# Later turns, a later first head and attention squares in SBUF in a hybrid decoder layer on one core

## The chip, the cores and the metric

The kernel runs on one NeuronCore of one Trainium2 chip. Its five instruction engines are named as in the profile: PE (TensorE, matrix products), DVE (VectorE), ACT (ScalarE), POOL (GpSimd) and SP (SyncE, which issues most DMAs). The metric is the device time of one execution in microseconds (us). Times are medians of several runs, and the profile is of one more execution.

## The reference

One decoder layer on 1024 tokens of width 1024, all in float32. A first RMS norm feeds one input projection, whose columns are split between two groups of heads:

```python
h = rms_norm(x, norm1_w[l])
proj = h @ w_in[l]
da_q, da_k, da_v, dn_qkv, dn_z, dn_a, dn_b = jnp.split(proj, [...], axis=-1)

da_q = rms_norm(da_q.reshape(B, S, DA_HEADS, 2, DA_QK_DIM), q_norm_w[l])   # 4 heads, two maps of 64
da_k = rms_norm(da_k.reshape(B, S, DA_HEADS, 2, DA_QK_DIM), k_norm_w[l])
da_o = diff_attention(da_q, da_k, da_v, lam)       # (softmax(q1 k1^T) - lam softmax(q2 k2^T)) v, causal
da_o = rms_norm(da_o, da_out_norm_w[l]) * (1.0 - lam_init)

dn_qkv = causal_conv_silu(dn_qkv, conv_w[l])       # group B: gated DeltaNet, 4 heads of 128
dn_o = gated_delta_rule(dn_q, dn_k, dn_v, g, beta) # chunked scan over the sequence
dn_o = rms_norm(dn_o, dn_out_norm_w[l]) * jax.nn.silu(dn_z...)

x = x + jnp.concatenate([da_o, dn_o], axis=-1) @ w_out[l]
h = rms_norm(x, norm2_w[l])
x = x + jnp.square(jax.nn.relu(h @ w_up[l])) @ w_down[l]
```

## The kernel before

The tokens are eight tiles of 128. Large products are made in float32 accuracy from rounded parts: each operand is split into a high part (`wH`, `hH`) and the rest (`wL`, `hL`), and three matmuls are added up. The kernel has four parts in time: norm, gates and convolution inputs up to about 226 us; an interleaved part up to about 600 us; the MLP's first matrix; the MLP's second.

The interleaved part is what the change touches. It runs these streams beside each other:

- `da_units()`: the projections of group A in six units of eight token tiles: keys, queries, values of heads 0 and 1 (`g` = 0), then of heads 2 and 3 (`g` = 1). A tile's product `ps_qk` is 24 matmuls (L1077 to L1079). For keys and queries ACT squares it (L1095) and copies it to `qn` (L1096), DVE sums the squares (L1098) and scales them (L290), POOL takes the power (L291), and DVE multiplies `qn` in place (L1102). The row is then put on the list `late`, with the time at which the planner expects it ready.
- `da_turns()`: takes the first of `late`, transposes it on PE into a PSUM bank (`ps_qkt`, L1038 and L1039), scales and splits it on ACT and DVE (`qa`, L1042 and L1043) and stores it to `qk_d` in DRAM by a DMA that POOL issues (L1044).
- `scan()` and `scan_out()`: the DeltaNet scan over eight chunks. A step has three groups of four products into `ps_A` (L928, L940, L951), with DVE or ACT between them (L932, L942, L957). `scan_out` makes a chunk's output from two more groups into one PSUM bank (`ps_o`, L980 and L987), evacuated by DVE (L981, L989). Operands come back from DRAM by SP's DMAs: `pka` (L920, two buffers), `pkb` (L970, five buffers, one per head) and `zgt` (L972). Its output goes out through POOL (`mixn_d`, L1001).
- `scores()`: loads a head's keys (`KS`, four DMAs, L1128), values (`vt`, L1135) and each tile's queries (`qa` and `qb`, four DMAs, L1143 and L1144), makes the scores `ps_sc` (L1203, L1204) and, on DVE and ACT, the two softmaxes `pexp` (L1214, L1215) and their difference (L1226).
- `values()`: transposes `pexp` (`ps_at`, L1248), copies it (L1250), multiplies by the values (`ps_o`, L1260), copies the result to `om` (L1269), squares that with a sum (L1270) and normalises it. The 32 outputs (4 heads, 8 tiles) each pass here.
- `mixed()`, `outproj()` and what follows: transposes of the mixed heads (`ps_tr`, L298), the output projection (`ps_op`, L1350 to L1352), the second norm.

The order on PE is written by a planner, the class `Interleave`, at build time. Each stream is a generator that yields the time from which it may go on, and the stream of the lowest priority number that may go on is run. Time moves on by assumed PE durations (`flow.pe`), and `flow.chain` books assumed durations on the other engines. PE's instructions stand in exactly this order (`tc.manual_schedule(engines={T.engine})`). The other engines' orders in this part, SP's DMA issues and POOL's among them, are not the planner's: the framework's scheduler makes them from the recorded program. At run time each engine works through its list in order and waits for what it needs.

Two PSUM banks, named `px`, are shared by the turned rows, the transposed `pexp`, the products with the values and the transposed mixed rows. The planner books a bank as free again after the copy that empties it. Before the change, the square of L1270 wrote its unused output into another part of the same bank, behind that copy:

```python
sq = po[:, P:2 * P]
S.copy(om, po[:, :P])
S.activation(sq, om, AF.Square, scale=ri[:, 0:1], accum_out=so)
...
t = flow.chain(act(P))
flow.hold(r, t)
```

Of the kernel before, what the change touches and what calls it, by code (L numbers as in the profile page):

```python
# [9 lines left out]
F32 = mybir.dt.float32  # L10
# [8 lines left out]
P = 128  # L19
# [12 lines left out]
MARGIN = 0.25  # L32
SCAN_START = 18000.0
MIX_T = 5000.0
DMA_T = 2500.0
AHEAD = 2

# [74 lines left out]
def vec(n, extra=0.0):  # L112
    return "V", 68.0 + 1.045 * n + extra


def powr(n):
    return "G", 180.0 + 285.0 * n
# [3 lines left out]
def tile_hymba_layer(  # L121
# [718 lines left out]
    for h, hf, q2 in skew(dn_proj(0)):  # L840
# [5 lines left out]
        sq = ta("kn", 2)  # L846
# [204 lines left out]
    def da_units():  # L1051
        todo = [(g, kind) for g in range(2) for kind in (1, 0, 2)]

        w = load_unit(w_units[2 * todo[0][1] + todo[0][0]]), unit_time()
        for g, kind in todo[1:]:
            quarters.plan(w_units[2 * kind + g])
        for k0 in (4, 0):
            for n in range(2):
                quarters.plan(w_halves[n], k0, 4)
        quarters.load()  # L1060
        quarters.load()
        freed = [0.0, 0.0]
        n = 0
        for i, (g, kind) in enumerate(todo):
            (wh, wl), wt = w
            for j in range(NT):
                tb = NT - 1 - j if i == len(todo) - 1 else j
                if j == 0:
                    if i + 1 < len(todo):
                        w = quarters.unit(256, KB)  # L1070
                    else:
                        pre.append(quarters.unit(512, 4))
                sl = slice(tb * P, (tb + 1) * P)
                yield max(freed[n % 2], wt[0] if j == 0 else 0.0), None
                ps = pj.tile([P, 512], F32, tag="pj", name="ps_qk")
                for k in range(KB):
                    T.matmul(ps[:, :256], hH[:, k, sl], wh[:, k, :], start=(k == 0), stop=False)  # L1077
                    T.matmul(ps[:, :256], hH[:, k, sl], wl[:, k, :], start=False, stop=False)  # L1078
                    T.matmul(ps[:, :256], hL[:, k, sl], wh[:, k, :], start=False, stop=(k == KB - 1))  # L1079
                    if k % 2 == 1:  # L1080
                        flow.pe(6 * TR)
                        if k < KB - 1:
                            yield wt[k // 2 + 1], None
                while len(late) > 2:
                    yield flow.now + 50, None
                qn = sd.tile([P, 256], F32, tag="qn", name="qn", bufs=4)
                if kind == 2:
                    newest["ACT"] = S.copy(qn, ps[:, :256])
                    st = nc.gpsimd.dma_start(v_d[g, tb], qn.rearrange("p (h e) -> p h e", h=2))
                    if g == 1:  # L1090
                        prefetch_x()
                    freed[n % 2] = flow.chain(act(256))
                else:
                    sq = ps[:, 256:512]
                    S.activation(sq, ps[:, :256], AF.Square)  # L1095
                    newest["ACT"] = S.copy(qn, ps[:, :256])  # L1096
                    sn = sd.tile([P, 4], F32, tag="sn", name="sn", bufs=2)
                    V.tensor_reduce(sn, sq.rearrange("p (a d) -> p a d", d=DQK), axis=AX.X, op=ALU.add)  # L1098
                    rn = sd.tile([P, 4], F32, tag="rn", name="rn", bufs=2)
                    rstd(rn, sn, 1.0 / DQK, EPS, sd, "rnt", 4)  # L1100
                    qv = qn.rearrange("p (a d) -> p a d", d=DQK)
                    V.tensor_tensor(qv, qv, rn.unsqueeze(2).broadcast_to([P, 4, DQK]), ALU.mult)  # L1102
                    t = flow.chain(act(256))
                    flow.chain(act(256), start=t - flow.HOP)
                    freed[n % 2] = t = flow.chain(vec(256), start=t - flow.HOP)
                    t = flow.chain(vec(4), powr(4), vec(256), start=t - flow.HOP)
                    late.append((g, kind, tb, qn, t))
                quarters.block()
                if i == len(todo) - 1:
                    over.add(tb)  # L1110
                n += 1
                state["units"] = n
            if kind == 2:
                while state["turned"] < 2 * NT * (g + 1):
                    yield flow.now + 50, None
                state["da"] = g + 1
                state["da_t"] = flow.now + 3000
        sdctx.close()
        pctx.close()
        state["proj"] = True  # L1120

    def load_head(h, pool):

        KS = []
        for m in range(2):
            k = pool.tile([P, SEQ], F32R, tag=f"KS{m}", name=f"KS{m}")
            for s in range(2):
                nc.sync.dma_start(k[HF[s]].bitcast(F32).rearrange("p (b t) -> p b t", t=P),  # L1128
                                  qk_d[h // 2, 1, :, HF[h % 2], s, m * P:(m + 1) * P].rearrange("b p t -> p b t"))
            KS.append(k)  # L1130
        return KS

    def load_v(h, pool):
        vt = pool.tile([P, NT, P], F32, tag="vt", name="vt")
        nc.sync.dma_start(vt, v_d[h // 2, :, :, h % 2, :].rearrange("t p e -> p t e"))  # L1135
        return vt
# [14 lines left out]
    def scores():  # L1151
        heads, npe, nsc = {}, 0, 0
        while state["da"] < 1:
            yield flow.now + 300, None
        heads[0] = load_head(0, ap), load_v(0, ap)
        q = load_q(*order[0])
        yield state["da_t"] + 3000, None
        for u, (h, tb) in enumerate(order):
            if u >= NT - 3 and 1 not in heads and state["scan"] or h == 1 and 1 not in heads:

# [71 lines left out]
    def values():  # L1232
        for _ in order:
            while not ready or ready[0][5] > flow.now:
                yield (flow.now + 100 if not ready else ready[0][5]), None
            h, tb, pe, ri, vt, _t = ready[0]
            if h == 2:
                while "ax" not in pools or len(rows_of) + len([x for x in loads if not x[3]]) > 1:
                    yield flow.now + 50, None
                rows_of[tb] = pools["ax"].tile([P, 512], F32, tag="mx", name="mx", bufs=2)  # L1240
                nc.sync.dma_start(rows_of[tb][:, 0:256], mixa_d[tb])
            ats = []
            for g in range(0, tb + 1, 4):
                r = yield from flow.bank("px")
                ng = min(4, tb + 1 - g)
                pt = bank_tile(px, r, "ps_at")
                for j in range(ng):
                    T.transpose(pt[:, j * P:(j + 1) * P], pe[:, (g + j) * P:(g + j + 1) * P], ident)  # L1248
                at = ap.tile([P, 512], F32, tag="at", name="at", bufs=2)
                newest["ACT"] = S.copy(at[:, :ng * P], pt[:, :ng * P])  # L1250
                ats.append(at)
                if g + 4 > tb:
                    ready.pop(0)
                flow.pe(ng * TR)
                t = flow.chain(act(ng * P))
                flow.hold(r, t)
            r = yield from flow.bank("px", at=t)
            po = bank_tile(px, r, "ps_o")
            for j in range(tb + 1):
                T.matmul(po[:, :P], ats[j // 4][:, (j % 4) * P:(j % 4 + 1) * P], vt[:, j, :],  # L1260
                         start=(j == 0), stop=(j == tb))
            if h < 2:
                om = ap.tile([P, P], F32, tag="om", name="om", bufs=2)
            else:

                om = rows_of[tb][:, h * P:(h + 1) * P]
            sq = po[:, P:2 * P]
            so = ap.tile([P, 1], F32, tag="so2", name="so2", bufs=2)
            S.copy(om, po[:, :P])  # L1269
            S.activation(sq, om, AF.Square, scale=ri[:, 0:1], accum_out=so)  # L1270
            f = ap.tile([P, 1], F32, tag="of2", name="of2", bufs=2)
            rstd(f, so, 1.0 / P, EPS, ap, "oft2", 1)
            V.tensor_tensor(f, f, ri[:, 0:1], ALU.mult)
            V.scalar_tensor_tensor(om, om, f, dawb, ALU.mult, ALU.mult)
            if h < 2:
                nc.gpsimd.dma_start(mixa_d[tb, :, h * P:(h + 1) * P], om)
            flow.pe((tb + 1) * MM)
            t = flow.chain(act(P))
            flow.hold(r, t)
            t = flow.chain(act(P, True), vec(1), powr(1), vec(1), vec(P, 60), start=t)  # L1280
            if h == 3:
                loads.append((rows_of.pop(tb), t, tb, 0))
        state["attn"] = True
# [644 lines left out]
```

## Time and profile before

| what | value |
|---|---|
| time, median of 3 runs | 1233.85 us (1232.64 to 1236.31) |
| time of the profiled execution | 1233.5 us |
| its span, first to last instruction | 1231.8 us |
| mean granted clock of PE | 0.998 |
| PE busy | 1215.3 us, 99% of the span |
| DVE, ACT, POOL busy | 829.9, 624.3, 151.3 us |
| data moved by DMA | 202.12 MB, mean 164 GB/s |

A row of waits reads: the waiting engine, the tile and line it was about to work on, an arrow, the engine, tile and line that released it, then the total in us, the number of times and the longest. A timeline row reads: start in us, duration in us, engine, line, operation, output tile and input tiles, and in brackets the idle time before it and what ended it. Matmuls are pipelined, so the durations of neighbours overlap. `SPq` is SP's queue of DMA issues. PE idle time is the complement of its busy time in a stretch.

### The profile page before, as it was taken

The page shows a single profiled execution, that of the slowest core. Times are in us where ns is not written, and L with a number is a line of the kernel's source. Part 1 is how long each engine was busy: PE and PEld are TensorE (multiplying, and loading weights), DVE is VectorE, ACT ScalarE, POOL GpSimd, SP SyncE. Part 2 cuts the span into 40 slices and gives each one's busy share as a digit, 9 for nine tenths or more (in the row PEclk, how much of TensorE's full clock was granted, in tenths as well). Part 3 has the DMA queues.
Part 4 walks back from the last instruction along what each step waited for, and adds up shares of the span by engine and source line. Part 5 has one row for each costly group of instructions (what it writes and reads, how often), then busy time and mean ns, then how long its engine had stood idle before and what let it go on. Part 6 is the DMA issues. An engine that isn't in the chain of part 4 may idle for free.

```text
span 1231.8 us, 18793 instructions
## 1 busy us (share of the span) xinstructions
PE 1215.3 (99%) x6791; PEld 1052.0 (85%) x6791; DVE 829.9 (67%) x1534; ACT 624.3 (51%) x1249; POOL 151.3 (12%) x215
## 2 busy tenths in 40 slices
PE   9999999998999999999999999999999999999998
PEld 8978888898999998888888888888888888888886
DVE  6868797665647657776799544565569755777543
ACT  6587553344356555566766544454564333333330
POOL 2411110033434421001200000000000000000000
PEclk9999999999999999999999999999999999999999
DMA  9334654378648855223437433444479655423401
GB/s 351 103 111 119 167 163 86 78 244 240 223 146 246 241 162 159 84 74 109 157 120 257 171 129 145 171 171 154 154 244 386 229 178 184 162 103 103 137 35 69
DMA packets 155973, 202.12 MB, mean 164 GB/s; under 512 B 37688, under 2 KB 110952, under 8 KB 155880
## 3 DMA queue, kind: packets, MB, share of 16 engines
q1 hardware_dynamic: 151256, 187.28, 46.9%
q0 software_dynamic: 4480, 13.64, 2.9%
q8 instruction: 54, 0.88, 0.3%
q14 instruction: 39, 0.32, 0.1%
q10 hardware_dynamic: 144, 0.00, 0.0%
HBM read 135.86 MB, written 65.01 MB: 163 GB/s over the span
## 4 chain that ended last, share of the span: by engine, by line
PE 90%; DMA 3%; DVE 2%; ACT 2%; issue 1%; SPq 1%; POOL 1%; DVEq 0%; ACTq 0%; POOLq 0%
PE X L1527 5%; PE X L1526 5%; PE X L1525 5%; PE X L1825 4%; PE X L1823 4%; PE X L1824 4%; PE ps_dn L265 3%; PE ps_dn L267 3%; PE ps_dn L266 3%; PE ps_qk L1077 3%; PE ps_qk L1079 3%; PE ps_qk L1078 3%; PE Y L1525 3%; PE Y L1526 3%; PE Y L1527 3%; PE ps_o L1260 2%
## 5 line engine op out<-in xcount | busy, mean ns | idle before, releaser
L1443 ACT CAST hH<-ur 128x1024 fp32r<-128x1024 f32 x56 | 58.9, 1051 | 173.4 <-PE Y L1824 89.4
L1444 DVE TENSOR_TENSOR hL<-ur,hH 128x1024 fp32r<-128x1024 f32 x56 | 68.4, 1223 | 78.9 <-ACT hH L1443 78.8
L1077 PE MATMUL ps_qk<-wH,hH 128*128 128x256 f32 x384 | 115.1, 300 | 0.0
L1079 PE MATMUL ps_qk<-wH,hL 128*128 128x256 f32 x384 | 109.0, 284 | 0.0
L1078 PE MATMUL ps_qk<-wL,hH 128*128 128x256 f32 x384 | 108.9, 284 | 0.0
L1444 DVE TENSOR_TENSOR op<-raw,op 128x1024 fp32r<-128x1024 f32 x48 | 58.7, 1224 | 74.1 <-PE X L1526 41.1
L1823 PE MATMUL X<-hH 128*128 128x512 f32 x224 | 87.1, 389 | 0.0
L1824 PE MATMUL X<-hL,hH 128*128 128x512 f32 x224 | 87.1, 389 | 0.0
L1825 PE MATMUL X<-hH,hL 128*128 128x512 f32 x224 | 87.1, 389 | 0.0
L265 PE MATMUL ps_dn<-hH,wH 128*128 128x512 f32 x192 | 76.0, 396 | 0.2 <-ACT cp L679 0.2
L266 PE MATMUL ps_dn<-hL,wH 128*128 128x512 f32 x192 | 75.8, 395 | 0.0
L267 PE MATMUL ps_dn<-hH,wL 128*128 128x512 f32 x192 | 75.5, 394 | 0.0
L1077 PEld LDWEIGHTS ps_qk<-wH,hH 128*128 128x128 f32 x384 | 74.0, 193 | 0.5 <-DVE sn L1098 0.2
L1078 PEld LDWEIGHTS ps_qk<-wL,hH 128*128 128x128 f32 x384 | 74.0, 193 | 0.2
L1079 PEld LDWEIGHTS ps_qk<-wH,hL 128*128 128x128 f32 x384 | 73.6, 192 | 0.0
L1444 DVE TENSOR_TENSOR hL<-dw,hH 128x1024 fp32r<-128x1024 f32 x56 | 68.2, 1219 | 1.4 <-ACT hH L1443 1.4
L1443 ACT CAST op<-raw 128x1024 fp32r<-128x1024 f32 x48 | 50.4, 1051 | 35.7 <-PE Y L1527 19.9
L1443 ACT CAST hH<-dw 128x1024 fp32r<-128x1024 f32 x56 | 58.7, 1049 | 10.9 <-DMA dw<-in_w_down_dram 5.5
L1215 ACT ACTIVATE pexp<-pexp,mx 128x128 f32<-128x128 f32 (+7 forms) x64 | 49.7, 777 | 24.5 <-DVE mx L1214 24.1
L683 DVE SCALAR_TENSOR_TENSOR cy<-cp,pv,cy 128x512 f32<-128x512 f32 x72 | 53.7, 747 | 8.4 <-ACT cy L681 7.5
L1350 PE MATMUL ps_op<-wH,hH 128*128 128x512 f32 x128 | 53.0, 414 | 0.0
L1352 PE MATMUL ps_op<-wH,hL 128*128 128x512 f32 x128 | 50.3, 393 | 0.0
(374 smaller groups left out, 3424.2 us busy)
## 6 DMA issues: line engine op xcount, KB each, us to landing
ur<-ud SPq DMA_DIRECT2D x28, 1024.0 KB, 5.3
raw<-in_w_up_dram SPq DMA_DIRECT2D x32, 512.0 KB, 4.2
dw<-in_w_down_dram SPq DMA_DIRECT2D x32, 512.0 KB, 6.5
wraw<-in_w_units_dram SPq DMA_DIRECT2D x48, 256.0 KB, 3.6
qk_d<-qa POOLq DMA_DIRECT2D x32, 256.0 KB, 4.2
ud<-ua SPq DMA_DIRECT2D x16, 512.0 KB, 4.3
ud<-s SPq DMA_DIRECT2D x16, 512.0 KB, 2.7
pka<-park_d SPq DMA_DIRECT2D x32, 192.0 KB, 4.3
```

The costliest lines, as they stand in the source:

```text
L265: T.matmul(ps, lh(k), rh(k), start=(k == 0), stop=False)
L266: T.matmul(ps, lh(k), rl(k), start=False, stop=False)
L267: T.matmul(ps, ll(k), rh(k), start=False, stop=(k == n - 1))
L1077: T.matmul(ps[:, :256], hH[:, k, sl], wh[:, k, :], start=(k == 0), stop=False)
L1078: T.matmul(ps[:, :256], hH[:, k, sl], wl[:, k, :], start=False, stop=False)
L1079: T.matmul(ps[:, :256], hL[:, k, sl], wh[:, k, :], start=False, stop=(k == KB - 1))
L1443: S.copy(dst[0], src)
L1444: V.tensor_tensor(dst[1], src, dst[0].bitcast(F32), ALU.subtract)
L1525: T.matmul(ps, op[0][:, k, cs], h[0][:, k, :], start=start and k == 0, stop=False, skip_group_check=True)
L1823: T.matmul(bank[t], v[0][:, j, sl], v[2][:, j], start=s0, stop=False, skip_group_check=True)
L1824: T.matmul(bank[t], v[0][:, j, sl], v[3][:, j], start=False, stop=False, skip_group_check=True)
L1825: T.matmul(bank[t], v[1][:, j, sl], v[2][:, j], start=False, stop=s1, skip_group_check=True)
```

## The change

Four edits in the interleaved part:

1. `late` may hold three rows, where it held two, before a unit's evacuation is recorded. There are four `qn` buffers before and after.
2. A row's planned time of readiness is put 1500 planner nanoseconds later (`TURN_T`).
3. After the first half of the projections is turned, `scores()` lets 4500 planner nanoseconds pass (`HEAD_T`) before it records the loads of the first head's keys, values and queries, and then 6000 more before the first scores. Before, it recorded the loads at once, and the first scores followed 3000 after `da_t`, which itself lies 3000 after the end of the turns.
4. The square of L1270 writes a new SBUF tile `osq2` of 128 x 128 with one buffer, instead of the PSUM bank.

```diff
 MIX_T = 5000.0
+TURN_T = 1500.0
+HEAD_T = 4500.0
 DMA_T = 2500.0
...
-                while len(late) > 2:
+                while len(late) > 3:
                     yield flow.now + 50, None
...
-                    t = flow.chain(vec(4), powr(4), vec(256), start=t - flow.HOP)
+                    t = flow.chain(vec(4), powr(4), vec(256), start=t - flow.HOP) + TURN_T
                     late.append((g, kind, tb, qn, t))
...
         while state["da"] < 1:
             yield flow.now + 300, None
+        yield flow.now + HEAD_T, None
         heads[0] = load_head(0, ap), load_v(0, ap)
         q = load_q(*order[0])
-        yield state["da_t"] + 3000, None
+        yield flow.now + 6000, None
...
-            sq = po[:, P:2 * P]
+            sq = ap.tile([P, P], F32, tag="osq2", name="osq2", bufs=1)
             so = ap.tile([P, 1], F32, tag="so2", name="so2", bufs=2)
             S.copy(om, po[:, :P])
             S.activation(sq, om, AF.Square, scale=ri[:, 0:1], accum_out=so)
```

## The prediction

> **What bounds the kernel.** I read the page first, then a table by stretches, then TensorE's own waits, and after that the chain and the timeline at the places that those waits name.
>
> ```profile
> span 1231.8 us, 18793 instructions
> PE 1215.3 (99%) x6791; PEld 1052.0 (85%) x6791; DVE 829.9 (67%) x1534; ACT 624.3 (51%) x1249; POOL 151.3 (12%) x215
> PE 90%; DMA 3%; DVE 2%; ACT 2%; issue 1%; SPq 1%; POOL 1%; DVEq 0%; ACTq 0%; POOLq 0%
> ...
> 226.00:364.00 138.00, 132.86 (x1160) 129.78 (x1159) 81.46 (x234) 57.47 (x168) 45.70 (x58) 0.99 0.62 192
> 364.00:460.00 96.00, 94.18 (x764) 92.11 (x763) 63.13 (x190) 59.49 (x165) 41.07 (x60) 1.00 0.71 215
> 460.00:600.00 140.00, 138.86 (x808) 120.39 (x807) 100.35 (x265) 86.33 (x224) 19.59 (x32) 1.00 0.35 104
> ```
>
> TensorE fills 99% of the span, so it is the bound, and no matmul is added or removed by this change (the built programs hold the same number of each). What can change is TensorE's idle time, and the change touches only the interleaved part, from about 226 to 600 us. Each row of the table is window, length, then busy time of PE, weight load, DVE, ACT and POOL, then clock, DMA share and GB/s. PE is idle for 138.00 - 132.86 = 5.1, 96.00 - 94.18 = 1.8 and 140.00 - 138.86 = 1.1 us: 8.1 us in all. That, and what a stop costs beside its idle time, is all that can be won.
>
> ```profile
> PE ps_o L980 <- DMA pkb<-park_d: 2.8, 1, 2.8
> PE ps_qkt L1038 <- DVE qn L1102: 1.8, 3, 1.0
> ...
> PE ps_qkt L1038 <- ACT ps_o L1270: 1.3, 2, 1.0
> ...
> PE ps_at L1248 <- ACT ps_o L1270: 0.8, 2, 0.7
> ...
> PE ps_sc L1204 <- DMA qb<-qk_d: 0.3, 1, 0.3
> PE ps_qkt L1038 <- DVE oft L290: 0.3, 1, 0.3
> ```
>
> These rows (total us, times, longest) name 7.3 of the 8.1 us. Three causes: a scan operand that lands late (2.8), normalised rows not ready when TensorE turns them (1.8 + 0.3: the row put down to `oft` is the turn of a late row too), and a PSUM bank still held by the attention's square (1.3 + 0.8).
>
> A stop costs more than its idle time, because matmuls overlap:
>
> ```profile
> 278.39 0.28 PE L1078 MATMUL ps_qk<-wL,hH 128*128 128x256 f32 x1
> 278.51 0.28 PE L1079 MATMUL ps_qk<-wH,hL 128*128 128x256 f32 x1
> 279.82 0.33 PE L1038 MATMUL ps_qkt<-ident,qn 128*128 128x128 f32 x1 [1.03 <-DVE qn L1102]
> ```
>
> Starts are 0.12 us apart, so the turn was due at 278.63 and came at 279.82: 1.19 us lost for 1.03 shown, 0.16 more per stop.
>
> **Rows planned later (TURN_T, three in waiting).** The planner puts 1.5 us more between a row's normalisation and its two transposes, and lets one more row queue (three, where two were allowed), so a unit need not wait at its end. In the built order of the changed program, the TensorE work between a unit's last matmul and its turn (rows 2 to 31, counted in matmuls times their start-to-start time in the trace: 0.12 us for a projection, 0.89 for a group of four scan products) is at least 6.26 us; before, it was at least 4.71. For the row above it was 18 projection matmuls, three scan groups and another turn, 4.95 us; now it is 36, three and one, 7.19 us. What it must cover is in the timeline:
>
> ```profile
> 273.47 0.28 PE L1079 MATMUL ps_qk<-wH,hL 128*128 128x256 f32 x1
> 277.63 0.60 POOL L1044 DMA_DIRECT2D qk_d<-qa  x1 [5.55 <-DVE rnt L290]
> 278.26 1.05 POOL L291 TENSOR_TENSOR rn<-rnt,neghalf 128x4 f32<-128x4 f32 x1
> 279.34 0.43 DVE L1102 TENSOR_TENSOR qn<-qn,rn 128x256 f32<-128x256 f32 x1
> ```
>
> The unit ended at 273.47, the row was ready at 279.77: 6.30 us, now under 7.19. The same count for the other late rows comes out safe too, the closest by a few tenths. So the four stops go: 1.8 + 0.3 + 4 x 0.16 = **2.7 us won**. Bounds: 0 (DVE and POOL come later by as much) to 2.7.
>
> **Squares in SBUF.** The square's output moves out of the bank, so the bank is free after the copy alone:
>
> ```profile
> 369.16 0.26 ACT L1269 COPY om<-ps_o 128x128 f32<-128x128 f32 x1
> 369.89 0.40 PE L1204 MATMUL ps_sc<-KS,qb 128*128 128x512 f32 x1
> 370.18 0.62 ACT L224 CAST wH<-wraw 128x512 fp32r<-128x512 f32 x1
> 370.70 0.37 ACT L1270 ACTIVATE ps_o<-om,ri 128x128 f32<-128x128 f32 x1
> 371.00 0.19 ACT L1270 ACTIVATION_READ_ACCUMULATOR ps_o<-om,ri 128x1 f32 x1
> 371.25 0.33 PE L1038 MATMUL ps_qkt<-ident,qn 128*128 128x128 f32 x1 [0.96 <-ACT ps_o L1270]
> ```
>
> The copy was done at 369.42, before TensorE wanted the bank at about 370.1; the square, behind a weight rounding on ACT, held it until 371.19. All four such stops end so: 1.3 + 0.8 + 4 x 0.16 = **2.7 us won**. Bounds: 0 (the copy or the next row is late instead) to 2.7. On ACT it costs this:
>
> ```profile
> L994 ACT ACTIVATE osq<-oc,small x32: 389/402/412, 261.5 to 350.4; 128x128 f32<-128x128 f32 x32
> L1270 ACT ACTIVATE ps_o<-om,ri x16: 366/372/377, 370.7 to 495.0; 128x128 f32<-128x128 f32 x16
> ```
>
> The scan's square of the same shape writes SBUF and takes a median of 402 ns, the attention's into PSUM 372. 32 squares x 30 ns = 1.0 us of ACT, which is busy 59 of 96 us in its fullest stretch. I take 0 on the path; bounds 0 to 1.0. The one buffer is written by ACT alone, in order, so nothing waits for it. The Trainium skill, "ScalarE: Activation LUTs" (its note that ScalarE to PSUM is faster than to SBUF), advises the opposite destination; the two rows above agree with its sign, and by it alone the edit would lose 1.0 us. Its own caveat, that TensorE must not need the PSUM, is what decides here.
>
> **First head's keys later (HEAD_T).** The wait it bears on is the dearest:
>
> ```profile
> 282.91 3.86 DMA qk_d<-qa
> 286.84 0.69 SPq L1128
> ...
> 288.92 0.63 SPq L1128
> ...
> 289.66 7.24 DMA pkb<-park_d
> 296.94 1.35 PE ps_o L980 x6
> ...
> DMA to landing us min/median/max: 2.1/4.3/6.8
> ...
> 297.00:298.30 1.30, 1.30 (x7) 1.18 (x8) 0.00 (x0) 0.00 (x0) 0.00 (x0) 0.82 0.93 296
> 298.30:301.30 3.00, 3.00 (x16) 3.00 (x16) 2.07 (x6) 0.38 (x2) 0.60 (x1) 0.51 0.44 148
> ...
> 280.50:284.00 3.50, 3.50 (x33) 3.50 (x32) 3.14 (x12) 1.01 (x3) 1.81 (x4) 1.00 0.99 360
> ```
>
> The last turned key row is stored at 282.91 and lands at 286.8; SP then issues the four key loads (L1128), and the scan's `pkb` loads behind them land 7.24 us after issue, where their median is 4.3. TensorE stops for 2.8 us (2.97 with the refill), and afterwards its granted clock is 0.51 for 3 us: 14 matmuls start 0.21 instead of 0.12 us apart or slower, about 1.4 us more. So this stop costs 4.4 us.
>
> But the delay is on the planner's clock, and only TensorE's order is taken from the planner. SP's is made by the scheduler. In the built order of the changed program the four key loads stand where they stood: after three groups of `pkb` and `zgt` loads, directly ahead of the four `pkb` loads of the same chunk. What moves is TensorE: the first score matmul comes after 672 projection matmuls instead of 636 (4.3 us later), and from the previous chunk's second product to this chunk's first there are 6.4 us of work instead of 5.7. The last key row is turned 2.2 us later by the order, of which 1.19 are the stop that goes; its store stands one normalisation further back on POOL. So keys and `pkb` land at about the same time as before, and TensorE wants them about 0.8 us later: I take a stop of 2.0 us, **0.8 us won**. Whether the clock still falls lies between two rows: after the 1.03 us of idle at 279.82 it stayed at 1.00 (last row), after 2.81 it fell. 2.0 is nearer to 2.81, so I leave the 1.4 us in. Bounds: 0 to 4.4.
>
> The Trainium skill, "TensorE: Matmul & The Clock Gate" (Part 1), says that the clock halves after an idle window of about 3.4 us. Here 2.81 us sufficed, so the measurement decides against that figure; by the rule a stop of 2.0 would keep the clock, which is rival 4.
>
> **New waits.** All streams are shuffled by a few us. In the built order six distances of the scan are short now: three times a chunk's second output product follows its first by 2.4 to 2.7 us (3.1 at the least before), and three times the next scan step follows by 3.1 to 3.3 (3.2 at the least before, mostly 4 to 6). They need DVE in time, which is busy 81 of 138 us there.
>
> ```profile
> 278.11 1.12 DVE L957 SCALAR_TENSOR_TENSOR S<-S,elast,ps_A 128x128 f32<-128x128 f32 x4 [0.71 <-PE ps_A L951]
> ```
>
> One such group ahead in DVE's queue is 1.1 us; I take one, **1.0 us lost**. Bounds: 0 to 6.6 (all six).
>
> **The sum.** 2.7 + 2.7 + 0.8 - 1.0 = 5.2 us won. The profiled execution took 1233.5 us (1.7 around its span), the median of the runs is 1233.85, 0.35 above. 1233.85 - 5.2 = **1228.6 us**. From about 440 us on the two TensorE orders hardly differ, and after 600 not at all. About 0.3%, 3.7 us, is what a measurement can tell from no change.
>
> **Rivals.**
> 1. The keys do get out of the way: `pkb` lands in time, and the clock holds. 2.7 + 2.7 + 4.4 - 1.0 = 8.8: 1225.0 us. For it: the stop is a matter of 2 us. Against: SP's order. That this edit does not do what it says stands in the forecast; here it does. Chance 0.15.
> 2. The waits come back elsewhere: 3 to 8 us of new stops, at the six tight places and at score, transpose and value products, which now start 4.3 us late and catch up within 20 us. 1230.6 to 1235.6, about 1232. For it: DVE and ACT are two thirds busy between 364 and 460. Against: the least distance before a turn grows by 1.5 us. Chance 0.22.
> 3. Slower: scan loads late. SP is in order; the first head's query loads, which wait for the ninth and tenth turned rows, stand ahead of the next chunks' loads, and the tenth comes 2.2 us later. If the first product (L980) of chunks 4 to 7 then stops as chunk 3's did, 4 x 3.0 = 12.0 us replace the 1.0: gain 6.2 - 12.0, so 1239.7 us. It decides from the fourth such stop (9.9 us of loss needed). Against: chunk 4's first product itself comes 4.8 us later in the order. Chance 0.13.
> 4. The forecast, but the clock holds through the shorter stop: 5.2 + 1.4 = 6.6, so 1227.2 us. For it: 1.03 us did no harm; against: 2.81 did. By the Trainium skill's "TensorE: Matmul & The Clock Gate" this is the outcome. Chance 0.09.
> 5. The forecast, with the 32 slower squares on the path: 5.2 - 1.0 = 4.2, so 1229.6 us. Against: none of TensorE's waits ends at the scan's squares. By the Trainium skill's "ScalarE: Activation LUTs" this is the direction. Chance 0.03.
>
> The forecast, 1227 to 1230.1, has the rest, 0.38. Range: 1224.5 (rival 1 with little new) to 1235.5 (rival 2's end), leaving out rival 3 and little else. Faster 0.38 + 0.15 + 0.09 + 0.03 = 0.65; same 0.22; slower 0.13.
>
> **What would show it.** In the profile after: no L1270 among TensorE's releasers; `qn` under 0.5 us; an idle of 1.5 to 2.5 us at L980 with the four L1128 issues still just ahead of `pkb`, and the clock row beside it. PE idle between 226 and 600 should be near 3.5 to 4.5 us. Wrong if new releasers of over 3 us appear, if the L980 stop is gone or grown, or if the clock falls elsewhere.

## The result

The changed kernel takes 1231.17 us (median of 10 runs, 1228.79 to 1233.16), the kernel before, run beside it, 1234.11 us (10 runs). The ratio is 0.9975 with an interval of [0.9965, 0.9985]: 2.9 us or 0.25% won. The forecast was 1228.6 us, a gain of 5.2. So the sign was right and the time lies inside the range, but the gain is little more than half of the forecast, within the 0.3% that the prediction called no change, and the time is the one that rival 2 gave (1230.6 to 1235.6).

The profiled execution took 1231.23 us. In the changed file the line numbers are higher by 2 up to the start of `scores()` and by 3 after the wait added there. First the page, as before: span, PE's busy time and the chain.

```profile
span 1229.5 us, 18782 instructions
...
PE 1214.4 (99%) x6791; PEld 1051.3 (86%) x6791; DVE 829.1 (67%) x1534; ACT 624.4 (51%) x1249; POOL 152.7 (12%) x215
...
PE 90%; DMA 4%; DVE 3%; ACT 1%; issue 1%; SPq 0%; POOL 0%; POOLq 0%; DVEq 0%; ACTq 0%
```

The same matmuls fill the same time; 2.3 us of span are gone. The table by stretches tells where (window, length, busy time of PE, weight load, DVE, ACT, POOL, then clock, DMA share, GB/s):

```profile
226.00:364.00 138.00, 135.73 (x1197) 132.77 (x1196) 84.67 (x240) 57.49 (x169) 47.85 (x60) 1.00 0.64 194
364.00:460.00 96.00, 92.95 (x746) 90.59 (x746) 63.77 (x191) 62.29 (x168) 40.53 (x58) 1.00 0.73 218
460.00:600.00 140.00, 138.91 (x810) 120.56 (x809) 99.82 (x261) 85.28 (x224) 20.02 (x32) 1.00 0.34 102
```

PE's idle time went from 5.1 to 2.3 us in the first stretch, rose from 1.8 to 3.1 in the second, and stayed at 1.1 in the third: 6.4 us, where 8.1 were and 3.5 to 4.5 had been forecast. PE's waits name it:

```profile
PE ps_sc L1206 <- DMA qa<-qk_d: 1.6, 1, 1.6
...
PE ps_o L982 <- DMA pkb<-park_d: 1.4, 2, 1.0
PE ps_sc L1207 <- DMA qb<-qk_d: 1.3, 2, 0.8
...
PE ps_sc L1206 <- DVE qa L1045: 0.6, 1, 0.6
...
PE ps_sc L1206 <- DVE mx L1217: 0.4, 1, 0.4
```

Every stop behind a late row (`qn`) and behind the square has gone, the one at `pkb` has shrunk from 2.8 to 1.0 (and 0.4 in the last chunk, at 338 us), and the clock holds: no half-speed stretch up to the last microsecond. In their place stand five stops at scores, 3.9 us where there was one of 0.3. Three of them wait for loads of queries (0.8 us at 373, 1.6 at 394, and 0.5 at 565, where the 0.3 stood before); two are put down to DVE (0.6 at 372 and 0.4 at 548). The longest one, on SP, in the chain that ended last, and on PE:

```profile
379.96 2.64 SPq L1130 DMA_DIRECT2D KS<-qk_d  x4
...
383.37 2.09 SPq L1028 DMA_DIRECT2D acc<-in_x_dram  x1
385.56 1.36 SPq L1145 DMA_DIRECT2D qa<-qk_d  x1
```
```profile
386.47 0.19 PE ps_sc L1207
386.66 0.25 SPq L1145
...
387.61 6.39 DMA qa<-qk_d
```
```profile
297.28 1.22 PE L982 MATMUL ps_o<-S,pkb 128*128 128x128 f32 x6 [0.99 <-DMA pkb<-park_d]
...
394.13 0.44 PE L1206 MATMUL ps_sc<-KS,qa 128*128 128x448 f32 x1 [1.64 <-DMA qa<-qk_d]
```

There are two buffers of queries, so a tile's loads can be issued only after the scores of the tile before last. SP came to these loads at 385.56, behind the second head's keys and values and the residual, and waited there until those scores ended at 386.66: the loads ahead did not hold up the issue. The load that PE waited for, issued at 387.61, then took 6.39 us to land, where the median of this line's loads from 362 to 396 us is 2.8 from issue to landing. The DMA share from 390 to 393.4 us was 1.07, so the transfers in flight beside it are the likely cause, but no run tests that, and none gives the queries a third buffer.

### The profile page after: what moved, and what is told of

The parts are those of the page before. It is cut to its first block, busy times and chain, and to the rows that moved or that the text cites. A ratio compares the mean times of both kernels' runs of the same rounds, so it can differ in the third digit from the quotient of the medians.

```text
span 1229.5 us, 18782 instructions
## 1 busy us (share of the span) xinstructions
PE 1214.4 (99%) x6791; PEld 1051.3 (86%) x6791; DVE 829.1 (67%) x1534; ACT 624.4 (51%) x1249; POOL 152.7 (12%) x215
## 4 chain that ended last, share of the span: by engine, by line
PE 90%; DMA 4%; DVE 3%; ACT 1%; issue 1%; SPq 0%; POOL 0%; POOLq 0%; DVEq 0%; ACTq 0%
PE X L1530 4%; PE X L1528 4%; PE X L1529 4%; PE X L1827 4%; PE X L1826 4%; PE X L1828 4%; PE ps_dn L267 3%; PE ps_dn L269 3%; PE ps_dn L268 3%; PE ps_qk L1079 3%; PE ps_qk L1080 3%; PE ps_qk L1081 3%; PE ps_o L1263 3%; PE Y L1528 2%; PE Y L1530 2%; PE Y L1529 2%
```

## The experiments

Twelve kernels, each timed in five rounds beside the kernel before. "Idle" is PE's idle time from 226 to 600 us in the one profiled execution, worked out from three windows as above; "profiled" is the time of that execution; "clock" is where the granted clock fell to a half, and for how long (every execution also has a short stretch at its very end, left out here). The last column is the median less the median of before in the same rounds (1233.6 to 1234.5), in us; by the ratio it would differ by up to 0.8 (no_head: +1.9).

| kernel | edits | idle, us | clock at half from | profiled, us | median, us | ratio | against before |
|---|---|---|---|---|---|---|---|
| before | none | 8.1 | 297.8, 3.4 us | 1233.50 | 1233.6 to 1234.5 | 1 | 0 |
| after | all | 6.4 | nowhere | 1231.23 | 1231.17 | 0.9975 [0.9965, 0.9985] | -2.9 |
| squares | 4 | 9.1 | 297.4, 3.4 us | 1235.98 | 1233.39 | 1.0002 [0.9994, 1.0011] | -0.2 |
| turns | 1 and 2 | 11.9 | 381.9, 6.8 us | 1239.54 | 1238.71 | 1.0041 [1.0029, 1.0053] | +5.1 |
| head | 3 | 9.3 | 297.9, 3.4 us | 1235.58 | 1237.10 | 1.0027 [1.0017, 1.0038] | +3.5 |
| no_head | 1, 2, 4 | 9.9 | 383.3, 3.4 us | 1236.32 | 1236.25 | 1.0015 [1.0004, 1.0026] | +2.6 |
| no_turns | 3 and 4 | 5.8 | 298.3, 3.4 us | 1230.71 | 1232.34 | 0.9983 [0.9974, 0.9992] | -2.1 |
| no_squares | 1, 2, 3 | 9.6 | 298.3, 3.4 us | 1236.23 | 1234.33 | 0.9998 [0.9988, 1.0009] | -0.2 |
| squares_om3 | 4, third `om` | 6.0 | 299.7, 3.4 us | 1232.11 | 1230.36 | 0.9967 [0.9955, 0.9979] | -4.1 |
| turns_om3 | 1, 2, third `om` | 7.0 | nowhere | 1231.65 | 1233.25 | 0.9995 [0.9986, 1.0004] | -0.9 |
| no_head_om3 | 1, 2, 4, third `om` | 3.4 | nowhere | 1229.54 | 1229.61 | 0.9965 [0.9952, 0.9979] | -4.8 |
| after_om3 | all, third `om` | 7.7 | nowhere | 1231.60 | 1231.75 | 0.9983 [0.9975, 0.9992] | -2.6 |
| squares_om3_k3 | 4, third `om`, keys behind `pkb` | 5.6 | 308.7, 3.4 us | 1230.53 | 1231.59 | 0.9978 [0.9966, 0.9990] | -2.8 |
| after_pace7 | all, scores paced | 5.4 | 397.6, 3.4; 612.6, 10.2 us | 1239.27 | 1237.11 | 1.0026 [1.0015, 1.0036] | +2.6 |

The idle time of one execution foretells a median to some 2 us only (turns_om3 and head are the worst), and the profiled execution itself lies up to 2.6 us from its kernel's median (squares).

**One edit at a time.** The edits are those of the diff, alone.

> Edit 4 alone: the attention's squares go to SBUF, all else as before. Theory A (each edit takes away the stops named for it, and the delayed first head brings the new ones): the order on TensorE stays as before, the stops at the square (2.1 us idle, 4 times, 2.7 us with the refills) go, those at the late rows (2.1 us idle) and at the scan operand (2.8 us idle, granted clock 0.5 for some 3.4 us after it) stay: 1231.4 us against 1234.1. Theory B (stops only change their place, and the gain is that of the clock alone): other stops of about 2 us take their place, no change within 1 us.

The stops behind the square went, and nothing was won: -0.2. PE's waits, and then two lines of ACT, the copy into `om` and the scaling of a turned row:

```profile
PE ps_o L1260 <- DVE qa L1043: 1.3, 1, 1.3
PE ps_qkt L1038 <- ACT om L1269: 1.1, 1, 1.1
PE ps_sc L1203 <- DMA qa<-qk_d: 0.9, 1, 0.9
```
```profile
382.80 0.27 ACT L1269 COPY om<-ps_o 128x128 f32<-128x128 f32 x1 [1.92 <-DMA mixa_d<-om]
...
403.49 0.47 ACT L1042 ACTIVATE qa<-ps_qkt,qw 128x256 fp32r<-128x256 f32 x1 [1.10 <-DMA qk_d<-qa]
```

The copy that frees the bank itself waits, for the store out of `om` (L1276), which has two buffers; this is PE's stop of 1.1 us, at 383 us. Its stop of 1.3 us, at 404.5, comes from another store: there the scaling waits until an earlier turned row has left its tile `qa`, also of two buffers. The 0.9 us are at 553 us. The kernel before had shown the same wait of the copy, at 385.85 us, though no stop of PE came of it:

```profile
ACT om L1269 <- DMA mixa_d<-om: 1.0, 1, 1.0
```

> Edits 1 and 2 alone: rows planned 1.5 us later and three in waiting; first head and squares as before. Theory A: the late-row stops go (2.7 us); the scan operand's stop shrinks to about 1 us as in the changed kernel, since the order up to there is the same, and the clock holds (3 us more); the stops at the square stay, 2 us idle. About 1228.5 to 1230 us, TensorE idle between 226 and 600 near 4 to 5 us, no query load among its releasers above 1 us. Theory B: the scan operand's stop stays 2.8 us with a clock drop, 1233 us.

+5.1, which neither theory has, though the stop at `pkb` did shrink to 1.0 us, as theory A said. The same wait on ACT, and what it does to PE:

```profile
383.16 0.27 ACT L1269 COPY om<-ps_o 128x128 f32<-128x128 f32 x1 [5.24 <-DMA mixa_d<-om]
```
```profile
384.00 0.47 PE L1038 MATMUL ps_qkt<-ident,qn 128*128 128x128 f32 x1 [4.33 <-ACT ps_o L1270]
```

PE's row names the square. It is the last writer of the bank, but it was late only because the copy ahead of it had waited 5.2 us for a store.

> Edit 3 alone: first head planned 4500 later; rows and squares as before. Theory A: the key loads keep their place in SP's queue, so the stop at the scan operand stays at 2.8 us with its clock drop, and the scores, which start later and catch up, wait for their query loads: 2 to 4 us of new idle at the score matmuls. 1236 to 1238 us. Theory B (the delay of the first head is what takes the scan operand's stop away): that stop is under 1.2 us, no clock drop, 1230 us.

+3.5. The stop at `pkb` stays at 2.7, the clock falls as before, and the waits behind the square grow from 2.1 to 3.7 us:

```profile
PE ps_at L1248 <- ACT ps_o L1270: 2.4, 5, 0.9
...
PE ps_qkt L1038 <- ACT ps_o L1270: 1.3, 2, 0.8
```

That is 1.2 us more idle in all, in the fastest of the kernel's seven executions, which is 2.1 us above the profiled one of before. The other 1.4 of the 3.5 us lie in executions without a profile, so most of the cost is open. Scores wait for query loads for 0.2 us only: theory A's time came, but not by its way.

**One edit left out.**

> The changed kernel without edit 3: rows later, squares in SBUF, first head recorded at once as before. Theory A: the query-load stops at the score matmuls (3.3 us idle between 364 and 460 in the changed kernel) go, the rest stays as in the changed kernel: about 1227 to 1228.5 us. Theory B: the query-load stops belong to the denser order as such and stay, or the scan operand's stop comes back with the clock drop: 1231 us or more.

+2.6. The stops at scores went, as theory A said (0.6 us are left), but without the later first head the copy into `om` stops PE for 2.8 us at 382 us, and the clock falls:

```profile
PE ps_qkt L1038 <- ACT om L1269: 4.2, 3, 2.8
```

> The changed kernel without edits 1 and 2 (rows planned as before, two in waiting), so the later first head and the squares in SBUF together. Theory A (the late first head is what lets the other edits keep their gains): only the four stops at late rows come back, 2.7 us, so about 1233.5 where before takes 1233.6; qn is again among TensorE's releasers with about 1.8 us, the pkb stop stays near 2.7, L1270 is gone. Theory B (each edit has its own price, and the prices add up): squares alone was -0.2 and the later head alone +3.5, so about 1236.9.

-2.1, 1232.34 us, where theory A gives -0.1 against before and theory B +3.3: neither came. The late rows and the `pkb` stop are back as foretold:

```profile
PE ps_o L980 <- DMA pkb<-park_d: 2.6, 1, 2.6
...
PE ps_qkt L1038 <- DVE qn L1102: 1.5, 3, 1.0
```

But the stops at scores are down to 0.6 us, all behind 550 us. The query stops at 373 and 394 us of the changed kernel are thus in neither no_head nor no_turns: they need the later rows and the later head together.

> The changed kernel without edit 4 (squares in the PSUM bank as before). Theory A: the four stops behind the square come back and nothing else, 1231.2 + 2.7 = about 1233.9, with L1270 among the releasers at about 2 us. Theory B: turns alone was +5.1 and the later head alone +3.5, so about 1242. A third possibility: the single long stop of turns alone (4.3 us behind a square, with the clock down for 6.8 us) is there again, then about 1238.

-0.2, 1234.33: theory A's time, and the third possibility is out too. The waits behind the square are back, and those at scores are there as in the changed kernel:

```profile
PE ps_sc L1203 <- DMA qa<-qk_d: 3.2, 3, 1.7
...
PE ps_at L1248 <- ACT ps_o L1270: 1.2, 5, 0.4
...
PE ps_qkt L1038 <- ACT ps_o L1270: 0.7, 1, 0.7
```

Not all of theory A's picture came: the stop at `pkb` is 2.0 us here and the clock falls behind it, where the changed kernel has 1.0 and no fall. Theory B is out: the three edits alone sum to -0.2 + 5.1 + 3.5 = +8.4 us, together they give -2.9. They share something.

**The shared thing: om's store.** One number is changed; where edit 4 is in, the square's unused output is bfloat16 to make room (the square takes 403 ns with it, 402 without):

```diff
-                om = ap.tile([P, P], F32, tag="om", name="om", bufs=2)
+                om = ap.tile([P, P], F32, tag="om", name="om", bufs=3)
...
-            sq = ap.tile([P, P], F32, tag="osq2", name="osq2", bufs=1)
+            sq = ap.tile([P, P], mybir.dt.bfloat16, tag="osq2", name="osq2", bufs=1)
```

> Squares alone (edit 4), with a third buffer for the attention's result om; the square's unused output is bfloat16 to make the room. Theory C (squares alone won nothing because the copy into om waits for the store out of om, so the bank is held by the copy instead of by the square): the waits on om's copy (1.1 us) and most of the new 3 us go, about 1231 (2.5 us won over before). Theory D (any change of the bank's timing only moves the stops to the next late thing): the same total of stops elsewhere, 1233 to 1234.

1230.36 us, 4.1 won where squares alone won 0.2. From 364 to 460 us PE now idles 0.3 us: the 1.1 us at the copy are gone, and the 1.3 us at the turned row with them. What is left is mostly what this edit does not touch:

```profile
PE ps_o L980 <- DMA pkb<-park_d: 2.7, 1, 2.7
PE ps_qkt L1038 <- DVE qn L1102: 1.7, 3, 1.0
```
```profile
364.00:460.00 96.00, 95.67 (x778) 94.14 (x777) 64.26 (x195) 61.49 (x169) 41.59 (x61) 1.00 0.71 217
```

> Edits 1 and 2 alone (squares in the PSUM bank, the first head as before) with a third om buffer; TensorE's order is the same as in turns. Theory C (turns alone was slow because the copy into om waited 5.2 us for the store out of om, which held the bank and stopped TensorE for 4.3 us, after which the clock was halved for 6.8 us): the long stop and the clock's fall go, 1238.7 - 4.3 - about 2 to 3.4 = 1231 to 1232.5; the short stops behind the square (L1270) stay, 1 to 2 us. Rival (the bank was held by the square, and POOL's queue, not the buffer, is late): the stop stays over 3 us, 1237 or more.

1233.25 us, 5.5 less than turns with the same order on PE. The 4.3 us stop and the clock's fall are gone; the short stops behind the square stay, as theory C said, though the time is 0.75 us above its bracket:

```profile
PE ps_qkt L1038 <- ACT ps_o L1270: 1.5, 4, 0.7
PE ps_at L1248 <- ACT ps_o L1270: 1.0, 2, 0.7
```

> The changed kernel without the later first head, with a third om buffer (and a bfloat16 unused output of the square to make the room). Theory C (om's store, not the earlier scores themselves, made the stop of 2.95 us and two smaller ones on L1269): these go, with the clock's fall behind the long one, 4.2 + 0.5 for the refills and up to 1.4, so about 1231. Theory D (with scores that early the turned rows, transposes and copies jam in any case): another stop of 2 us or more between 370 and 400 us, 1234 to 1236.

1229.61 us, 6.6 less than no_head: the lowest median of all, though squares_om3's interval overlaps its own. PE idles 3.4 us in the whole part and only 1.8 in its first stretch:

```profile
226.00:364.00 138.00, 136.21 (x1195) 132.88 (x1195) 86.38 (x249) 60.26 (x176) 46.88 (x59) 1.00 0.64 196
```
```profile
PE ps_o L980 <- DMA pkb<-park_d: 0.8, 2, 0.6
```

> The changed kernel with a third om buffer. Theory C: no stop of the changed kernel ends at om, so the buffer brings nothing here, 1231.2 within 0.7. Theory D': om's stores do hold ACT in the changed kernel too, where other things queue behind the copy, and 1 to 2 us are won: 1229 to 1230. Worse than 1232.5 would mean that the scheduler's new order alone costs something.

1231.75, the same as the changed kernel: theory C. There no stop ended at `om`, and the stops at scores remain:

```profile
PE ps_sc L1206 <- DMA qa<-qk_d: 2.5, 2, 1.8
```

With three `om` buffers squares (-4.1) and turns (-0.9) make -5.0, and both together measure -4.8: they add up, if the buffer alone is worth nothing. The kernel before with a third `om` buffer and nothing else was not run, so the buffer's own share is open. The later first head then costs some 2 us (no_head_om3 to after_om3, -4.8 to -2.6, intervals that just overlap). With two buffers it pays 5.5 us (no_head to after): in no_head copies into `om` wait 4.5 us for its store, in the changed kernel none does. The store is not the only link, though. On top of the later head, edit 4 is worth 5.6 us (head +3.5, no_turns -2.1), and in head no copy waits for `om`'s store; there the edit takes away the 3.7 us of waits behind the square, and the rest is open.

**The stops at scores.** A planner rule keeps a tile's scores back until the query buffer has been free for 7 us:

```diff
+            while u > 1 and flow.now < done[u - 2] + PACE:
+                yield done[u - 2] + PACE, None
             KS, vt = heads[h]
```

> The changed kernel with one more rule for the planner: a tile's scores may not start before 7 planner us after the scores of the tile before last ended, which is when its query buffer came free. In the built order the first eight tiles' scores are then 8.5 to 20 us apart from tile to next but one, where they were 6.4 to 24. Theory A: the stops at scores that wait for query loads or their buffers (0.8, 1.0, 1.9 and two of 0.6 us start to start, 3.6 us for the three largest) go, about 1227.6. Rival: the catching up was needed, and values and softmax come late at the end of the scan instead, 1231 or more.

Inside the part it did what it should by half: the stops at scores fell from 3.9 to 1.8 us and PE's idle time from 6.4 to 5.4. But the time rose to 1237.1. The rival's kind of price, in another place: behind the part, PE stands 7.8 us, up to 617.5, at the second norm's last tile, and the clock is halved for 10.2 us from 612.6 on. The chain that ended last runs there through a store to `acc_d` that takes 5.85 us to land.

```profile
PE ps_tr L1463 <- DVE hL L307: 7.8, 1, 7.8
...
PE ps_sc L1209 <- DMA qa<-qk_d: 1.8, 1, 1.8
```

**The keys behind pkb.**

```diff
-            nc.sync.dma_start(pkb[h], park_d[h, c, :, 3:5, :])
+            newest["pkb", c] = nc.sync.dma_start(pkb[h], park_d[h, c, :, 3:5, :])
...
-        heads[0] = load_head(0, ap), load_v(0, ap)
+        with tc.issue_after(newest["pkb", 3].ins):
+            heads[0] = load_head(0, ap), load_v(0, ap)
```

> Squares with three om buffers, and the first head's four key loads put behind the pkb loads of chunk 3 in SP's queue (an ordering edge, no planner change). Theory A (pkb is late because it stands behind the keys, which wait for the last key row's store): the stop of 2.9 us at L980 and the clock's fall after it go, 2.9 to 4.3 us against the same kernel without the edge, so about 1226.8. Rival (pkb lands late because so much is in flight then, as the DMA share of 0.94 to 0.99 says): a stop of 1.5 to 2.5 us stays, 1229 to 1230.4. The keys are needed only about 70 us later, so no score should wait for them.

1231.59 us, nothing won over squares_om3 (its 0.9967 against 0.9978; the intervals overlap). The order is the one wanted, and chunk 3 has no stop at `pkb`, but 1.6 us came at chunk 4, and the clock fell there. Chunk 4's loads were issued from 302.61 us on, behind loads of queries in SP's queue, though the products that had read their buffers (L987) had ended at 300.2. Neither theory foretold that:

```profile
288.46 1.83 SPq L970 DMA_DIRECT2D pkb<-park_d  x4
290.59 0.69 SPq L1128 DMA_DIRECT2D KS<-qk_d  x1
```
```profile
PE ps_o L980 <- DMA pkb<-park_d: 1.6, 2, 1.3
```

## Why the prediction was right, and where it was not

Its sum was 2.7 + 2.7 + 0.8 - 1.0 = 5.2. Term by term in the two profiled executions, at 0.16 us per stop beside the idle time:

- **Rows planned later, 2.7: as forecast in the trace.** All four stops are gone in the changed kernel, and without edits 1 and 2 they come back (no_turns). What the prediction left out is that the edits reorder the streams at 380 us too: alone they cost 5.1 us, and win 0.9 once the store is out of the way. And on top of the other two they are worth only 0.8 us of time (no_turns -2.1, all four -2.9, intervals that overlap): with the later head they bring the stops at scores. (The two sums for the late row, 4.95 and 7.19 us, differ by 2.24 where 18 more matmuls at 0.12 make 2.16; nothing hangs on it.)
- **Squares in SBUF, 2.7: as forecast in the trace; the size is not settled.** no_squares is 2.7 us slower against before than the changed kernel (-0.2 to -2.9), but its profile also has 1.0 us more at `pkb` and a fall of the clock, and elsewhere the edit was worth from 0.2 (squares) to 5.6 us (head to no_turns). The lower bound, "0 (the copy or the next row is late instead)", is what the edit alone gave, and for that reason: the copy was late, and so was another row. The slower destination cost nothing that can be seen: the squares take 402 ns as forecast, and ACT's busy time is 624.4 us where it was 624.3. The caveat that the prediction takes from the Trainium skill, "ScalarE: Activation LUTs", is narrower on the page, which speaks of TensorE needing most of the PSUM; here it was one bank.
- **First head's keys later, 0.8: wrong size, wrong edit.** The four key loads keep their place ahead of `pkb`, as predicted. But the stop fell from 2.81 to 0.99 us and the clock held: with 0.4 at a later chunk, 3.0 + 1.4 - 1.2 - 0.6 = 2.7 us won. `pkb` landed 0.3 us later than before, but PE came to it 2.2 us later (296.29 against 294.13). The prediction saw that PE's side moves and put it at 0.8. And it is not edit 3 that moves it: head keeps 2.7 us, while every kernel with edits 1 and 2 has 0.6 to 2.0 at that place. That the clock holds is rival 4. But 1.4 us for the clock is read from one execution of before, and not every one pays it (the last section).
- **New waits, 1.0: the term that was mis-sized.** I had put one DVE group on the scan's tight products; of that 0.2 us came (`S`). In its place PE waits at scores: 3.9 us and five refills, less the 0.5 that was there before, is 4.2; with the 0.2 and its refill 4.6, and 0.6 more at L300, where the stop at 605 us is 0.74 us instead of 0.15. 5.2 instead of 1.0. Rival 2 named the place ("score, transpose and value products, which now start 4.3 us late and catch up within 20 us") and not the mechanism: two query buffers, filled by loads that go out only once earlier scores have ended and then land late.

2.7 + 2.7 + 2.7 - 5.2 = 2.9. The medians differ by 2.9, the two profiled executions by 2.3, so the sum is good to some 0.6 us only. The forecast came as near as it did by luck: two errors of 1.9 and 4.2 us had opposite signs. Its larger fault is that it priced the edits one by one: it saw no link between them, and the runs show that edits 1, 2 and 4 without edit 3 lose 2.6 us.

Of the signs that it named, three came (no square among the releasers, no `qn`, the keys still ahead of `pkb`); the stop at L980 was shorter than its 1.5 to 2.5, the idle time was 6.4, above its 3.5 to 4.5, and new releasers of over 3 us did appear. Rival 1 is not what happened, and where its order was forced the gain was not there. Rival 3, later scan loads, did not come.

## What to carry to other kernels

When PE waits for a bank, follow the engine that frees it one step further: here the copy was waiting for a DMA store out of a two-buffer tile, and one more buffer of 512 bytes per partition brought 3.9 us on top of edit 4 (squares to squares_om3), more than the whole change. Look for such waits in the profile before, even where nothing stops there yet. Price coupled edits together: count which tiles' stores and loads cross the place to which each edit moves work, and test them by leaving one out as well as by doing one alone. An edit that helps because it moves work away from a jam can turn into a cost once the jam is removed, as the later head seems to here.

## What the runs showed of the hardware

**The clock falls by windows, not by the length of a stop.** In every profiled execution the half-speed stretches between 205 and 640 us last 3.41 us or a multiple (6.83, 10.24). So I laid windows of 3.41 us on the raster that the clock's own changes give and took PE's busy time in each. Before, then no_turns, then squares_om3_k3 (a window and the next, with PE's clock third from the end):

```profile
294.41:297.82 3.41, 0.88 (x5) 0.76 (x6) 0.74 (x4) 0.00 (x0) 0.75 (x1) 1.00 1.05 338
297.82:301.23 3.41, 3.41 (x17) 3.41 (x17) 2.07 (x6) 0.34 (x1) 0.60 (x1) 0.50 0.50 162
```
```profile
294.89:298.31 3.42, 1.74 (x13) 1.64 (x13) 0.61 (x3) 0.00 (x0) 0.11 (x1) 1.00 1.07 361
298.31:301.72 3.41, 3.17 (x16) 2.90 (x15) 2.57 (x8) 1.64 (x4) 0.60 (x1) 0.50 0.61 174
```
```profile
305.26:308.67 3.41, 1.78 (x12) 1.35 (x11) 2.42 (x9) 0.00 (x0) 1.58 (x2) 1.00 1.03 331
308.67:312.09 3.42, 3.42 (x17) 3.42 (x18) 1.02 (x2) 0.34 (x1) 0.00 (x0) 0.50 1.02 333
```

A window in which PE is busy for 0.88, 1.74 or 1.78 of 3.41 us is followed by one at half speed. Two that are not, from no_squares and from the changed kernel (its 1.64 us stop):

```profile
373.42:376.83 3.41, 1.89 (x12) 1.60 (x13) 2.00 (x8) 2.56 (x10) 1.18 (x2) 1.00 0.73 241
376.83:380.24 3.41, 3.41 (x29) 3.32 (x29) 2.42 (x10) 2.69 (x9) 2.03 (x3) 1.00 0.05 14
```
```profile
392.29:395.71 3.42, 1.78 (x13) 1.53 (x11) 1.50 (x4) 1.28 (x4) 1.02 (x2) 1.00 0.96 359
395.71:399.12 3.41, 3.41 (x30) 3.35 (x28) 2.31 (x7) 2.27 (x4) 1.49 (x2) 1.00 0.88 241
```

In the fourteen profiled executions, between 205 and 640 us, a clock at full speed fell after each window with a busy share of up to 0.51, never after one of 0.55 or more, and at 0.52 once and once not. So in these traces a share of about one half in a fixed window decides. Two stops of 0.34 and 1.29 us in one window sufficed (squares_om3_k3); one of 1.73 us with most of it in one window did not (no_squares). The Trainium skill, "TensorE: Matmul & The Clock Gate" (Part 1), says that the window is 3413 ns long and free-running: the traces agree, with 3.41 us. That a whole idle window is needed they do not bear out. The raster lies differently in each execution, so the same stop can bring a fall in one and none in the next. In 27 of the 90 executions of the kernel before that were timed beside the other kernels the mean granted clock was 1.000, which leaves no room for a half-speed stretch of 3.41 us; their median is 1233.3 us, that of the 39 with 0.998 or less is 1234.4. The prediction's choice between the clock falling and holding at 2.0 us of idle was therefore a matter of chance.

**A store holds its tile long.** Two rows of turns: the time from issue to landing of the stores of `om` between 374 and 392 us, and their median over the kernel (64 KB each, the last number).

```profile
DMA to landing us min/median/max: 4.6/6.0/7.4
...
mixa_d<-om POOLq DMA_DIRECT2D x16, 64.0 KB, 3.1
```

The one of 7.4 us, issued at 375.63, is the one that the copy of 383.16 waited for.
